# Output projection as seven block products in the MLP's pipeline, with sums and differences on GpSimd

## The chip, the cores and the metric

The kernel runs on one core of a Trainium2 chip. The metric is the device time of one execution in microseconds, as the median of several runs. The engines are TensorE (PE in the profile, PEld for its weight loads), VectorE (DVE), ScalarE (ACT), GpSimd (POOL) and SyncE (SP), which here only issues transfers. Each engine works through its own queue in order; semaphores tie the queues together.

## The reference, cut to what matters

Two decoder layers, model width D = 1024, T = 512 tokens, float32. In each layer:

```python
h = rmsnorm(x, norm_mix)
z = h @ w_in                       # attention, mLSTM and gate columns
mixed = sigmoid(g_a) * (att @ w_att_branch) + sigmoid(g_m) * (hm @ w_m_branch)
x = x + mixed @ w_out              # 1024 x 1024
u = relu(rmsnorm(x, norm_ffn) @ w_ff1)
x = x + (u * u) @ w_ff2            # 1024 -> 4096 -> 1024
```

The output projection is the line with `w_out`. It stands between the gated sum of the two branches, whose second product is the one with `w_m_branch`, and the norm ahead of the MLP.

## The kernel before, in words

**Precision.** Every float32 operand is split in two: a high part, the operand copied into the matmul type (on ScalarE), and a low part, operand minus high part (on VectorE). A product is three matmuls, high by high, high by low and low by high (`mm3`). In the names, `wh` and `wl` are the halves of a weight tile, `uh` and `ul` those of an activation tile of the MLP, `a` and `i` activation tiles.

**The mixer** (`mixer`, one call per layer) multiplies the normed input with pieces of `w_in`, does attention and the mLSTM beside that, and ends with the branch products. Weights come as 128x512 tiles of 256 KB through `chunk` (L164 to L192): a transfer into pool `wraw` (three buffers), the split on ScalarE (L190) and VectorE (L191) into pool `wsp` (four). `feat_steps` and `tok_steps` list the matmul groups of a product with the features or the tokens on the rows of its result; `weave` puts a list of side work between them at given places. For `w_m_branch` each result tile goes through `ev_m` (L786): VectorE multiplies it with the sigmoid (L788), adds the other branch (L789), and the sum is split. The output projection (L796 to L803) takes two column halves of eight weight tiles by four token blocks by three matmuls, 192 in a layer, and adds to the residual `xtok` (L799). The first half of the next norm's transposes is woven into its second column half.

**The MLP** (`mlp`) has four parts of 1024 hidden columns. FF1 of a part is four slots of 48 matmuls (`First`), each with two transfers of 512 KB (tile `f`). FF2 of a part is a 1024 x 1024 x 512 product done by 2 x 2 blocks with seven products in place of eight (`slots_of`): p1 to p7, each 24 matmuls in two halves of 12. It needs sums and differences of blocks. Of the weight blocks b11, b12, b21, b22 (512 KB tiles `raw`, two per block): d1 = b12 - b11, t2 = b22 - d1, b12 becomes b22 - b12, and b21 becomes b21 - t2. Of the activation blocks a11, a12, a21, a22 (tiles `u`, sums in `s`): s1 = a21 + a22, s2 = s1 - a11, s3 = a11 - a21, s4 = a12 - s2. All of these are VectorE operations on 128x1024 (`w_minus` L829, `u_op` L833). `w_split` (L820) and `u_split` (L837) make the halves, `gain` (L845) adds a product to the residual.

**The order.** The slots of all parts are one list. Ahead of half i of the list, the loads, splits and differences of the halves up to i + 5 are issued (`prepare`), so a weight half is prepared two and a half slots early. In parts 0 to 2 FF1 slots of the next part stand between FF2 products; in part 3 there are only the seven products. Memory comes from pools that are opened in turn at the start of `mixer` and of `mlp`, and are given back at its end; the pools of the next phase lie over those of the last, so that the first tile in such a place waits for the last use of what lay there.

Of the kernel before, what the change touches and what calls it, by code (L numbers as in the profile page):

```python
# [16 lines left out]
P = 128  # L17
# [11 lines left out]
NEG = -1.0e30  # L29
LN_EXP = "natural_log_exp_and_others"  # L30
# [3 lines left out]
def hybrid_kernel(ctx, tc, x, norm_mix, w_in, att_q_norm, att_k_norm, att_sinks, m_gate_bias,  # L34
# [87 lines left out]
    def g_ffn(l, k):  # L122
        return gcol[:, 16 + 8 * l + k:17 + 8 * l + k]
# [234 lines left out]

    def mixer(l, norm, late, order, phase):
# [4 lines left out]
        pool(phase, "act", 32)  # L364
        pool(phase, "tmp", 18)
        mid = pool(phase, "mid", 1)
# [132 lines left out]
        att_acts = [(slot(F32R), slot(F32R)) for _ in range(4)]  # L499
# [284 lines left out]
        mixed = [None] * KT  # L784
        for g in range(2):
            def ev_m(m, ps, g=g):  # L786
                i = 4 * g + m
                ve.tensor_tensor(sgm[g][m], sgm[g][m], ps, op=ALU.mult)  # L788
# [7 lines left out]
        for j in range(2):  # L796
            def ev_x(b, ps, j=j):
                xb = xtok[b // 2][j][:, b % 2, :]
                ve.tensor_tensor(xb, xb, ps, op=ALU.add)  # L799

            weave(tok_steps(mixed, lambda k, j=j: [w_out[l, k * P:(k + 1) * P, T * j:T * (j + 1)]], ev_x,
                            end_pair=j == 1),
                  norm.steps(0, 1.5, 0.5) if j else [])  # L803
        return norm

    def mlp(l, norm, late, phase):
# [22 lines left out]
        def w_minus(d, p, q):  # L829
            with tc.high_priority():  # L830
                ve.tensor_tensor(d, p, q, op=ALU.subtract)

        def u_op(d, p, q, op):  # L833
            with tc.high_priority():
                ve.tensor_tensor(d, p, q, op=op)
# [19 lines left out]
        class First:  # L855


            def __init__(self, part, q, which="f"):
                self.c0, self.q, self.which, self.w = 1024 * part + 256 * q, q, which, []

            def load(self, h):
                with tc.high_priority():
                    r = fr.tile([P, 4, 2 * P], F32, tag="f", name=nm("f"))
                    nc.sync.dma_start(r, w_ff1[l, 4 * h * P:4 * (h + 1) * P, self.c0:self.c0 + 2 * P]
                                      .rearrange("(k p) n -> p k n", p=P))
                self.w.append(w_split(r))

            def step(self, k):
                if k == 0:
                    self.ps = banks(self.which)  # L870
                hi, lo = self.w[k // 4]
                for m in range(2):
                    c = slice(m * P, (m + 1) * P)
                    mm3(self.ps[:, m, :], hi[:, k % 4, c], lo[:, k % 4, c], acts[k][0], acts[k][1], k == 0, k == KT - 1)
# [8 lines left out]
        def new_u():  # L883
            return [uraw.tile([P, 4, T], F32, tag=f"u{g}", name=nm("u")) for g in range(2)]
# [7 lines left out]
        def first_slot(part, q, u):  # L892
            f = First(part, q)
            return Slot(f.load, lambda h: [f.step(k) for k in range(4 * h, 4 * h + 4)], lambda: f.evac(u))
# [26 lines left out]
        def slots_of(part, u, nxt):  # L921
# [3 lines left out]
            end = part == 3  # L925
            b11, b12, b21, b22, t2 = ([None] * 2 for _ in range(5))

            def load(to, h, i, j):
                with tc.high_priority():
                    r0 = 1024 * part + (4 * i + 2 * h) * P  # L930
                    to[h] = raws.tile([P, 2, T], F32, tag="raw", name=nm("raw"))
                    nc.sync.dma_start(to[h], w_ff2[l, r0:r0 + 2 * P, j * T:(j + 1) * T]
                                      .rearrange("(k p) n -> p k n", p=P))
# [15 lines left out]
            def w6(h):  # L949
                return t2[h], lambda: w_minus(b12[h], b22[h], b12[h])  # L950
# [7 lines left out]
            def w2(h):  # L958
                load(b21, h, 1, 0)
                return b21[h], lambda: w_minus(b21[h], b21[h], t2[h])  # L960
# [19 lines left out]

            p1 = product("x", True, w1, lambda: a11, [(0, 0, False)])
            p5 = product("y", True, w5, s1, [(1, 1, False)])
            p6 = product("x", False, w6, s2, [(0, 1, False)])
            p3 = product("y", False, w3, s4, [(0, 1, end)])
            p7 = product("x", False, w7, s3, [(1, 1, end), (1, 0, False)])
            p2 = product("f" if end else "y", True, w2, lambda: a12, [(0, 0, end)])
            p4 = product("y", True, w4, lambda: a22, [(1, 0, end)])
# [4 lines left out]


        us = [new_u()]
        f01 = [First(0, 0, "f"), First(0, 1, "x")]
        for h in range(2):
            for f in f01:
                f.load(h)
        weave([(0.5, lambda k=k, f=f: f.step(k)) for k in range(KT) for f in f01], late + [(4.5, norm.columns), (6.5, lambda: rowf.append(norm.along()))])
        for f in f01:  # L1000
            f.evac(us[0])
        slots = [first_slot(0, 2, us[0]), first_slot(0, 3, us[0])]
        for part in range(4):
            if part < 3:
                us.append(new_u())
            slots += slots_of(part, us[part], us[part + 1] if part < 3 else None)
        halves = [(s, h) for s in slots for h in range(2)]
        preps = list(halves)
        side = nnorm.steps(1, 0.5, 0.5) if nnorm else []

        def prepare(n):
            while preps and len(halves) - len(preps) < n:
                s, h = preps.pop(0)
                s.prep(h)

        steps = []
        for i, (s, h) in enumerate(halves):
            def go(i=i, s=s, h=h):
# [7 lines left out]
            last = i >= len(halves) - 4  # L1026
            steps.append((1.0 if last else 0.0, go))
        weave(steps, side)
# [6 lines left out]
    for l in range(DEPTH):  # L1035
        with ExitStack() as phase:
            norm = mixer(l, norm, late, order, phase)
        late = norm.steps(1, 1.5, 0.5)
        with ExitStack() as phase:
            norm = mlp(l, norm, late, phase)  # L1040
        late = norm.steps(0, 1.5, 0.5) if norm else []
        order = [4, 5, 6, 7, 0, 1, 2, 3]
# [40 lines left out]
```

## Time and profile before

| | |
|---|---|
| Time, median of 3 runs | 1337.89 us (1336.92 to 1338.45) |
| Profiled execution, span from first to last instruction | 1335.6 us |
| TensorE busy | 1312.4 us (98%) |
| VectorE busy | 926.3 us (69%) |
| ScalarE busy | 666.4 us (50%) |
| GpSimd busy | 106.7 us (8%) |
| Mean granted TensorE clock | 0.999 |

The profiled execution's own time is its span; the median of the timed runs is 2.3 us above it. In a row of a group, the numbers behind the bar are the busy time of the group in us, the mean of one instruction in ns, and the idle time of the engine ahead of it with what ended it. In a row of a list in time order, the first number is the start and the second the duration, both in us. In a row of a window, the numbers are its length, then busy time and instructions of PE, PEld, DVE, ACT and POOL, the granted clock, the DMA engines' busy share and GB/s. In a wait row they are the total, the times and the longest. Matmuls overlap in the pipeline, so the time between two starts is what one costs. Line numbers of the first kernel are one to eight off those of the changed one: its L46 is L45 here, L191 and L192 are L190 and L191, L796 the add that was L789, L821 and L822 are L825 and L826, L827 is L831, L831 is L835, L837 and L838 are L841 and L842, L860 is L864.

### The profile page before, as it was taken

What the parts mean: (1) busy time and instruction counts of PE and PEld (TensorE: products, weight loads), DVE (VectorE), ACT (ScalarE), POOL (GpSimd) and SP (SyncE); (2) the same over time, 40 slices, a digit from 0 to 9 for tenths busy, and PEclk for the clock granted to TensorE, in tenths of its full rate; (3) what the DMA queues carried; (4) which work ended last, traced back from release to release, by engine and by line L of the source; (5) the groups of instructions that cost most, each with busy time, mean ns of one, the idle gap of its engine ahead of it and who ended that gap; (6) DMA issues with size and microseconds to landing.
All of it is one profiled execution on the core that took longest, in us unless ns stands there. A gap on an engine that the chain in (4) does not pass through costs nothing.

```text
span 1335.6 us, 16885 instructions
## 1 busy us (share of the span) xinstructions
PE 1312.4 (98%) x6106; PEld 1078.1 (81%) x6106; DVE 926.3 (69%) x1409; ACT 666.4 (50%) x1201; POOL 106.7 (8%) x215
## 2 busy tenths in 40 slices
PE   8999999999999999999999999999999999999998
PEld 6877788888788888888888777888887888888886
DVE  4688764474576876868947887554646778678687
ACT  5458765544334344343554687554434444344343
POOL 4512310000000000000015013000000000000000
PEclk9999999999999999999999999999999999999999
DMA  5322122421523133131024221243216242322211
GB/s 151 108 72 72 56 79 74 140 95 64 189 95 126 63 127 125 64 119 46 34 65 123 67 71 64 72 122 96 99 54 207 73 132 81 125 95 95 95 48 63
DMA packets 87282, 125.02 MB, mean 94 GB/s; under 512 B 8216, under 2 KB 45184, under 8 KB 87200
## 3 DMA queue, kind: packets, MB, share of 16 engines
q1 hardware_dynamic: 86240, 123.30, 29.3%
q8 instruction: 48, 0.79, 0.2%
q10 hardware_dynamic: 576, 0.53, 0.1%
q0 software_dynamic: 384, 0.13, 0.1%
q14 instruction: 34, 0.28, 0.1%
HBM read 121.84 MB, written 2.10 MB: 93 GB/s over the span
## 4 chain that ended last, share of the span: by engine, by line
PE 88%; DVE 6%; ACT 4%; issue 1%; DMA 1%; POOL 0%; ACTq 0%; SPq 0%; DVEq 0%; POOLq 0%
PE mm L45 82%; PE aux L45 4%; PE aux L49 2%; ACT t L574 1%; DVE wl L191 1%; ACT wh L190 1%; DVE t L561 1%; DVE t L611 0%; DMA w<-in_w_in_dram 0%; DVE t L201 0%; ACT wh L825 0%; DVE t L538 0%; ACT junk L287 0%; DVE t L579 0%; DMA grow<-in_norm_mix_dram 0%
## 5 line engine op out<-in xcount | busy, mean ns | idle before, releaser
L45 PE MATMUL mm<-i,wh 128*128 128x512 f32 x1664 | 522.6, 393 | 2.1 <-DVE a L661 1.2
L45 PEld LDWEIGHTS mm<-i,wh 128*128 128x128 f32 x1664 | 307.7, 188 | 65.8 <-DVE a L661 2.0
L45 PE MATMUL mm<-i,wl 128*128 128x512 f32 x832 | 324.8, 390 | 0.0
L191 DVE TENSOR_TENSOR wl<-w,wh 128x512 fp32r<-128x512 f32 (+1 forms) x208 | 140.4, 677 | 131.7 <-ACT wh L190 126.8
L190 ACT ACTIVATE wh<-w 128x512 fp32r<-128x512 f32 (+1 forms) x208 | 127.2, 612 | 146.9 <-PE mm L45 123.8
L825 ACT ACTIVATE wh<-raw 128x1024 fp32r<-128x1024 f32 x112 | 118.3, 1056 | 151.9 <-PE mm L45 116.4
L45 PEld LDWEIGHTS mm<-i,wl 128*128 128x128 f32 x832 | 156.2, 188 | 33.0 <-issue 0.5
L45 PE MATMUL mm<-wh,uh 128*128 128x512 f32 x448 | 174.5, 389 | 0.0
L45 PE MATMUL mm<-wh,ul 128*128 128x512 f32 x448 | 174.3, 389 | 0.0
L45 PE MATMUL mm<-wl,uh 128*128 128x512 f32 x448 | 174.3, 389 | 0.0
L826 DVE TENSOR_TENSOR wl<-raw,wh 128x1024 fp32r<-128x1024 f32 x112 | 135.9, 1219 | 37.8 <-ACT wh L825 37.4
L45 PE MATMUL mm<-wh,i 128*128 128x512 f32 (+1 forms) x512 | 149.8, 371 | 0.4 <-ACT wh L190 0.4
L825 ACT ACTIVATE wh<-f 128x1024 fp32r<-128x1024 f32 x64 | 67.2, 1056 | 118.8 <-PE mm L45 92.3
L45 PEld LDWEIGHTS mm<-wh,i 128*128 128x128 f32 x512 | 92.7, 189 | 15.9 <-ACT wh L190 0.8
L826 DVE TENSOR_TENSOR wl<-f,wh 128x1024 fp32r<-128x1024 f32 x64 | 77.7, 1221 | 30.3 <-ACT wh L825 30.1
L45 PEld LDWEIGHTS mm<-wh,ul 128*128 128x128 f32 x448 | 84.1, 188 | 17.5
L45 PEld LDWEIGHTS mm<-wh,uh 128*128 128x128 f32 x448 | 84.1, 188 | 17.4
L45 PEld LDWEIGHTS mm<-wl,uh 128*128 128x128 f32 x448 | 84.1, 188 | 17.3
L45 PE MATMUL mm<-wl,i 128*128 128x512 f32 (+1 forms) x256 | 94.7, 370 | 0.0
L879 DVE SCALAR_TENSOR_TENSOR u<-mm,t 128x1024 f32<-128x1024 f32 x32 | 39.1, 1222 | 69.2 <-PE mm L45 69.1
L849 DVE TENSOR_TENSOR x<-x,mm 128x1024 f32<-128x1024 f32 x64 | 77.2, 1217 | 13.6 <-PE mm L45 13.6
L45 PE MATMUL mm<-wh,a 128*128 128x512 f32 x256 | 81.4, 393 | 0.0
(214 smaller groups left out, 1619.0 us busy)
## 6 DMA issues: line engine op xcount, KB each, us to landing
w<-in_w_in_dram SPq DMA_DIRECT2D x128, 256.0 KB, 2.6
f<-in_w_ff_dram SPq DMA_DIRECT2D x64, 512.0 KB, 3.7
raw<-in_w_ff_dram SPq DMA_DIRECT2D x64, 512.0 KB, 3.5
w<-in_w_out_dram SPq DMA_DIRECT2D x32, 256.0 KB, 2.5
w<-in_w_att_branch_dram SPq DMA_DIRECT2D x16, 256.0 KB, 2.5
w<-in_w_m_branch_dram SPq DMA_DIRECT2D x16, 256.0 KB, 2.5
w<-in_w_in_dram SPq DMA_DIRECT2D x16, 128.0 KB, 2.1
out_dram<-x SPq DMA_DIRECT2D x8, 256.0 KB, 2.2
```

Source lines behind the costliest of these rows:

```text
L45: return nc.tensor.matmul(*args, **kw)
L49: return nc.tensor.transpose(*args)
L190: sc.activation(wh[:, :off], raw[:, :off], AF.Copy)
L191: ve.tensor_tensor(wl[:, :off], raw[:, :off], f32(wh[:, :off]), op=ALU.subtract)
L561: ve.copy_predicated(dst, tri_i.unsqueeze(1).to_broadcast([P, 2, P]), p4[:, :, 1, :])
L574: sc.activation(s3[:, i, :], s3[:, i, :], AF.Exp, bias=m[:, i:i + 1], accum_out=den[:, i:i + 1])
L825: sc.activation(hi, r, AF.Copy)
L826: ve.tensor_tensor(lo, r, f32(hi), op=ALU.subtract)
L849: ve.tensor_tensor(xh, xh, ps, op=ALU.add)
L879: ve.scalar_tensor_tensor(dst, self.ps, 0.0, rowf[0].unsqueeze(1).to_broadcast([P, 2, T]), op0=ALU.max, op1=ALU.mult)
```

## The change

The output projection is taken out of `mixer` and put at the start of `mlp`, as a list of seven products through the same `slots_of`, with `mixed` in the place of `u` and `w_out` in the place of `w_ff2`. Its order is p1, p2, p5, p6, p3, p7, p4. `mixed` is two tiles of 128x4x512 in a new pool `half`, which lives through the whole kernel, holds the attention's split result in the mixer, and also holds `u` of parts 1 and 3. The last add of `mixed`, all weight differences and all activation sums go to GpSimd. The last half of the norm's transposes is woven into the projection's last product and the first half into the first FF1 slots, which therefore take their rows in the order 4 to 7, 0 to 3. The pools of both phases are opened in another order.

```diff
+    half = ctx.enter_context(tc.tile_pool(name="half", bufs=1, reuse_waits="tile"))
...
-        pool(phase, "act", 32)
+        pool(phase, "act", 24)
+        mid = pool(phase, "mid", 1)
         pool(phase, "tmp", 18)
-        mid = pool(phase, "mid", 1)
...
-        mixed = [None] * KT
+        mixed = halves_of()
         for g in range(2):
             def ev_m(m, ps, g=g):
-                i = 4 * g + m
                 ve.tensor_tensor(sgm[g][m], sgm[g][m], ps, op=ALU.mult)
-                ve.tensor_tensor(prod[i], prod[i], sgm[g][m], op=ALU.add)
-                mixed[i] = split(prod[i])
+                gp.tensor_tensor(mixed[g][:, m, :], prod[4 * g + m], sgm[g][m], op=ALU.add)
...
-        uraw = pool(phase, "uraw", 2)
-        raws = pool(phase, "raws", 8)
-        uspl = pool(phase, "uspl", 2)
-        spl = pool(phase, "spl", 5)
-        pool(phase, "tmp", 2)
-        fr = pool(phase, "fr", 3)
+        uspl = pool(phase, "uspl", 2)
+        pool(phase, "tmp", 2)
+        uraw = pool(phase, "uraw", 1)
+        fr = pool(phase, "fr", 3)
+        raws = pool(phase, "raws", 8)
+        spl = pool(phase, "spl", 5)
...
         def w_minus(d, p, q):
             with tc.high_priority():
-                ve.tensor_tensor(d, p, q, op=ALU.subtract)
+                gp.tensor_tensor(d, p, q, op=ALU.subtract)
 
         def u_op(d, p, q, op):
             with tc.high_priority():
-                ve.tensor_tensor(d, p, q, op=op)
+                gp.tensor_tensor(d, p, q, op=op)
...
+            def w6(h):
+
+                def then():
+                    w_minus(b12[h], b22[h], b12[h])
+                    if part is None:
+                        w4_diff(h)
+
+                return t2[h], then
...
+            if part is None:
+                return [p1, p2, p5, p6, p3, p7, p4]
...
+        run(slots_of(None, mixed), norm.steps(1, 0.5, 0.5), 2)
+        us = [new_u(0)]
+        f01 = [First(0, 0, "f"), First(0, 1, "x")]
+        for h in (1, 0):
+            for f in f01:
+                f.load(h)
+        weave([(0.5, lambda i=i, k=k, f=f: f.step(i, k)) for i, k in enumerate(LATE_FIRST) for f in f01],
+              norm.steps(0, 1.5, 0.5)
+              + [(4.5, norm.columns), (6.5, lambda: rowf.append(norm.along()))])
...
-            norm = mixer(l, norm, late, order, phase)
-        late = norm.steps(1, 1.5, 0.5)
+            mixed = mixer(l, norm, late, order, phase)
         with ExitStack() as phase:
-            norm = mlp(l, norm, late, phase)
+            norm = mlp(l, mixed, phase)
```

How the queues stand now is shown at three places of layer 0; layer 1 reads alike. First SyncE's queue, where the transfers of the mixer's last weights end and those of the output projection begin, before:

```order
L180 DMA w_633_3082<-in_w_m_branch_dram 128x512 [waits DMAHW7_49,DVE_49]
L180 DMA w_636_3100<-in_w_m_branch_dram 128x512 [waits DMAHW0_49,DVE_49]
L180 DMA w_649_3144<-in_w_out_dram 128x512 [waits DMAHW1_49,DVE_49]
L180 DMA w_653_3163<-in_w_out_dram 128x512 [waits DMAHW2_49,DVE_49]
L180 DMA w_656_3181<-in_w_out_dram 128x512 [waits DMAHW3_49,DVE_49]
```

and after:

```order
L181 DMA w_624_3083<-in_w_m_branch_dram 128x512 [waits DMAHW5_49,DVE_49]
L860 DMA f_700_3471<-in_w_ff1_dram 128x4x256 [waits PE_49,Pool_49]
L932 DMA raw_632_3139<-in_w_out_dram 128x2x512 [waits Pool_49]
L860 DMA f_703_3477<-in_w_ff1_dram 128x4x256 [waits Pool_49]
L932 DMA raw_633_3141<-in_w_out_dram 128x2x512
L860 DMA f_706_3483<-in_w_ff1_dram 128x4x256
L932 DMA raw_636_3148<-in_w_out_dram 128x2x512 [waits DMAHW6_49]
L932 DMA raw_637_3150<-in_w_out_dram 128x2x512 [waits DMAHW7_49]
L932 DMA raw_640_3157<-in_w_out_dram 128x2x512 [waits DMAHW0_49,Pool_49]
L932 DMA raw_643_3163<-in_w_out_dram 128x2x512 [waits DMAHW1_49,Pool_49]
```

Before, a tile of w_out waited for a buffer that VectorE's split three tiles earlier had freed. Now an FF1 tile stands ahead of the first one, and its wait on PE is for the second-last matmul of w_m_branch, which read the memory that this tile takes. raw_632 and raw_636 are the two halves of b11, raw_633 and raw_637 of b12, raw_640 and raw_643 of b21.

Second, ScalarE's queue from the split of the last w_m_branch tile on, before:

```order
L190 ACTIVATE wh_637_3102<-w_636_3100 128x512
L200 ACTIVATE a_617_3022<-a_281_1392 128x512
L200 ACTIVATE a_619_3028<-a_282_1394 128x512
L190 ACTIVATE wh_650_3146<-w_649_3144 128x512
L200 ACTIVATE a_621_3034<-a_283_1396 128x512
```

and after:

```order
L191 ACTIVATE wh_625_3085<-w_624_3083 128x512 [waits DMAHW0_49,DVE_49,PE_49]
L837 ACTIVATE uh_630_3135<-u_597_2943 128x1024 [waits Pool_49]
L837 ACTIVATE uh_650_3177<-u_598_2944 128x1024 [waits PE_49,Pool_49]
L821 ACTIVATE wh_634_3143<-raw_632_3139 128x1024 [waits DMAHW2_49]
L821 ACTIVATE wh_638_3152<-raw_636_3148 128x1024 [waits DMAHW6_49]
L821 ACTIVATE wh_641_3159<-raw_640_3157 128x1024 [waits DMAHW0_49]
L837 ACTIVATE uh_659_3222<-s_629_3134 128x1024 [waits DVE_49,PE_49,Pool_49]
L821 ACTIVATE wh_644_3165<-raw_643_3163 128x1024 [waits DMAHW1_49]
```

u_597 and u_598 are the two tiles of `mixed`, wh_650 (before) and wh_634 (after) the first split of w_out. Before, tiles of `mixed` and of the weights were split in turn, eight by eight; now a copy of the second half of `mixed`, which product 2 uses, stands ahead of the first weight split. uh_659 is the split of s1.

Third, GpSimd's queue in the same place, after:

```order
L831 TENSOR_TENSOR s_629_3134<-u_597_2943,u_598_2944 128x1024 [waits PE_49,Activation_49,Pool_49]
L831 TENSOR_TENSOR u_597_2943<-u_597_2943 128x4x256 [waits Pool_49]
L827 TENSOR_TENSOR raw_632_3139<-raw_633_3141,raw_632_3139 128x1024 [waits DMAHW4_49,DMAHW2_49,DVE_49]
L827 TENSOR_TENSOR raw_636_3148<-raw_637_3150,raw_636_3148 128x1024 [waits DMAHW7_49,DMAHW6_49,DVE_49]
L827 TENSOR_TENSOR raw_649_3175<-raw_646_3169,raw_632_3139 128x1024 [waits DMAHW2_49,Pool_49]
L827 TENSOR_TENSOR raw_633_3141<-raw_646_3169,raw_633_3141 128x1024
L827 TENSOR_TENSOR raw_640_3157<-raw_640_3157,raw_649_3175 128x1024 [waits DMAHW0_49,DVE_49,Pool_49]
L831 TENSOR_TENSOR s_629_3134<-s_629_3134,u_597_2943 128x1024 [waits DVE_49]
L827 TENSOR_TENSOR raw_656_3200<-raw_653_3194,raw_636_3148 128x1024 [waits DMAHW3_49,DVE_49,Pool_49]
L827 TENSOR_TENSOR raw_637_3150<-raw_653_3194,raw_637_3150 128x1024
L827 TENSOR_TENSOR raw_643_3163<-raw_643_3163,raw_656_3200 128x1024 [waits DMAHW1_49,Pool_49]
L831 TENSOR_TENSOR s_629_3134<-u_598_2944,s_629_3134 128x1024 [waits DVE_49]
```

Before, GpSimd had nothing to do from the end of the mLSTM to the next layer. Its queue now holds, in this order and behind the eight adds of `mixed`, s1, s3, d1 of both halves, t2, b12 and b21 of the first half, s2, t2, b12 and b21 of the second half, then s4.

More of the change, by code (lines that the diff above doesn't have):

```diff
@@ L29 @@
 NEG = -1.0e30
+LATE_FIRST = [4, 5, 6, 7, 0, 1, 2, 3]
 LN_EXP = "natural_log_exp_and_others"
@@ L991, in slots_of, with run, prepare, go @@
             return [p1, f[0], p5, p6, f[1], p3, p7, f[2], p2, f[3], p4]
[L994 to L1018, printed above, removed]
+        def run(slots, side, last):
+            halves = [(s, h) for s in slots for h in range(2)]
+            preps = list(halves)
+            def prepare(n):
+                while preps and len(halves) - len(preps) < n:
+                    s, h = preps.pop(0)
+                    s.prep(h)
+            def go(i, s, h):
+                if i == 0 and s.acts_:
+                    s.acts_()
                 prepare(i + 5)
```

75 lines of the change are left out of this document (42 added, 33 removed).

## The prediction

> **What bounds the kernel now.** I read the busy totals and the chain of waits first, then TensorE's own waits, then the stages that the change touches as windows.
>
> ```profile
> PE 1312.4 (98%) x6106; PEld 1078.1 (81%) x6106; DVE 926.3 (69%) x1409; ACT 666.4 (50%) x1201; POOL 106.7 (8%) x215
> PE 88%; DVE 6%; ACT 4%; issue 1%; DMA 1%; POOL 0%; ACTq 0%; SPq 0%; DVEq 0%; POOLq 0%
> PE aux L49 <- DMA grow<-in_norm_mix_dram: 5.3, 1, 5.3
> PE aux L49 <- DVE t L561: 3.8, 6, 1.2
> PE mm L45 <- DVE a L661: 1.2, 2, 0.6
> ```
>
> TensorE works 98% of the span and 88% of the chain is its own. Its longest wait is the first load (5.3 us); after that no releaser costs it more than 3.8 us over the whole run. So a matmul removed is worth its full pitch, and equally a wait put ahead of TensorE is paid in full. The pitch, from two MLP matmuls and the window of layer 0's output projection:
>
> ```profile
> 655.03 0.39 PE L45 MATMUL mm<-wh,uh 128*128 128x512 f32 x1
> ...
> 661.38 0.39 PE L45 MATMUL mm<-wl,uh 128*128 128x512 f32 x1
> 278.80:322.40 43.60, 43.60 (x198) 36.10 (x198) 28.45 (x45) 16.00 (x26) 0.00 (x0) 1.00 0.31 98
> 333.50:691.00 357.50, 356.27 (x1587) 293.27 (x1587) 267.17 (x257) 156.02 (x180) 0.00 (x0) 1.00 0.30 98
> ```
>
> Between the first two rows lie 28 pitches, 6.35 / 28 = 0.227 us. The output projection's 192 matmuls take 43.6 us with TensorE never idle; the MLP (third row) idles 1.2 us in 357.5.
>
> Why is there no gap where `mixed` ends and the projection starts? Its weights come in pieces of 256 KB, asked for well ahead:
>
> ```profile
> L180 SPq DMA_DIRECT2D w<-in_w_out_dram x16: 327/328/328, 278.7 to 319.6; - x16
> DMA to landing us min/median/max: 2.4/2.5/2.8
> ```
>
> Sixteen issues from 278.7 to 319.6 are one per 2.72 us, 2.5 us each to land, three buffers deep: the supply keeps pace with use.
>
> **The change, part by part. Removed:** 24 matmuls per layer (seven products of 24 for 192), 48 in all: 48 x 0.227 = **-10.9 us**. Everything else on TensorE stays in number.
>
> **Added: a cold start of the projection, twice.** By the order of SyncE's queue nothing of w_out is asked for before the second-last w_m_branch matmul, as an FF1 load stands ahead of it that waits for that matmul. Call the end of w_m_branch T. What a burst of 512 KB tiles gives is seen at the start of the MLP before:
>
> ```profile
> 338.50 1.58 SPq L932 DMA_DIRECT2D raw<-in_w_ff_dram  x3
> L932 SPq DMA_DIRECT2D raw<-in_w_ff_dram x3: 378/379/469, 338.5 to 339.6; - x3
> DMA to landing us min/median/max: 3.9/4.5/6.2
> GB/s 0 0 0 0 0 0 0 119 279 348 168 377 406 369 344 324 360 301 285 317 385 410 389 391 377 360 369 379 373 356 336 295 354 365 254 70 119 150 330 346
> ```
>
> The first tile takes 3.9 us and the third lands at 339.6 + 6.2 = 345.8; the last row (0.5 us a slice from 336) settles near 350 GB/s, 1.5 us a tile. I take 3.9 us and 1.6 for each further tile, from T - 0.2. The first w_out block is the second transfer: T+5.3. Its other half is the sixth, T+11.7, since FF1 tiles and b12 are interleaved; the eighth (first block of product 2) lands at T+14.9, the ninth at T+16.5. Each then needs its two halves made:
>
> ```profile
> L825 ACT ACTIVATE wh<-raw 128x1024 fp32r<-128x1024 f32 x112 | 118.3, 1056 | 151.9 <-PE mm L45 116.4 <-issue 20.9 <-ACT wh L825 9.9
> L826 DVE TENSOR_TENSOR wl<-raw,wh 128x1024 fp32r<-128x1024 f32 x112 | 135.9, 1219 | 37.8 <-ACT wh L825 37.4
> L831 DVE TENSOR_TENSOR raw<-raw,raw 128x1024 f32<-128x1024 f32 x64 | 76.9, 1222 | 1.2
> L835 DVE TENSOR_TENSOR s<-u,u 128x1024 f32<-128x1024 f32 x8 | 9.8, 1225 | 0.0
> L788 DVE TENSOR_TENSOR a<-a,mm 128x512 f32<-128x512 f32 x16 | 10.6, 682 | 0.7 <-PE mm L45 0.4
> ```
>
> The last gating product needs 2 x 0.68 (L788) behind T; the last `mixed` add follows on GpSimd at T+3.6, and ScalarE's copy of the second half of `mixed` stands ahead of the first weight split, 1.06 more. The first split then ends T+6.4, so TensorE stands about **6.5 us** instead of none. The second half of product 1 can run at 11.7 + 1.06 + 1.22 = T+14.0 and ends T+16.5; product 2 starts when 14.9 + 2.3 = T+17.2 and, its second split being queued behind the copy of s1 which itself needs product 1's buffer, ends T+22.6. Gapless the two would end at T+10.9: 11.7 us lost by loads and splits alone.
>
> **Moved: sums and differences to GpSimd.** Per layer 8 adds of 128x512 and 60 operations of 128x1024. The nearest rows:
>
> ```profile
> L466 POOL TENSOR_TENSOR t<-a 128x512 f32<-128x512 f32 x8 | 8.4, 1086 | 504.0 <-ACT a L378 504.0
> L492 POOL TENSOR_TENSOR rp<-a,ct 128x128 f32<-128x128 f32 x8 | 4.3, 536 | 0.0
> L466 POOL TENSOR_TENSOR t<-a x8: 1037/1040/1230, 35.5 to 699.7; 128x512 f32<-128x512 f32 x8
> ```
>
> 1.04 us for 512 columns alone; 128 to 512 columns adds 0.50, so 1024 lie between 1.04 + 0.67 = 1.7 and 2 x 1.04 = 2.1. I take 2.0, nearest to doubling, against 1.22 on VectorE. In the projection GpSimd's chain (s1, s3, two d1, t2, b12, b21, s2, t2, b12, b21, s4: twelve times 2.0 = 24 us) runs beside 38.1 us of matmuls. Walked with the landings above, and with both engines free of each other, only s4 is late: product 3 starts about 1.8 to 2.4 us late, and product 4 ends at T+52.1. Less 168 x 0.227 = 38.1 that is **14.0 us of stall a layer**.
>
> **Costed at nothing.** The transposes and splits of the second norm move from FF1 and the old second column half into product 4 and FF1: the same number, and FF1 starts with the columns whose splits come from product 4. Their cover is product 4's 5.45 us (24 x 0.227); without it FF1's first matmul would wait for one ScalarE and one VectorE step, about 1.3 us by the L190 and L191 rows below. SyncE's fourth FF1 tile now queues behind five FF2 tiles which wait for buffers that the projection's splits free; those come free two products earlier, 10.9 us, against four landings of 1.6.
>
> **Do they run beside each other?** This is the largest unknown, and one place of the trace speaks on it:
>
> ```profile
> 711.35 0.18 DVE L405 TENSOR_TENSOR ig<-kvi,gbias 128x16 f32<-128x16 f32 x1
> 711.39 1.04 POOL L469 TENSOR_TENSOR t<-kvi 128x512 f32<-128x512 f32 x1 [10.49 <-ACT kvi L381]
> 711.44 1.02 DVE L407 TENSOR_TENSOR fg<-kvi,gbias 128x16 f32<-128x16 f32 x1
> L407 DVE TENSOR_TENSOR fg<-kvi,gbias x2: 1023/1024/1024, 50.6 to 711.4; 128x16 f32<-128x16 f32 x2
> ```
>
> Twin operations of 16 columns: the one begun before GpSimd's takes 0.18 us, the one begun just behind it 1.02, until GpSimd is done, and so in both layers. L466 in its turn reaches 1.23 us beside a VectorE split. I read that a VectorE operation with two inputs in SBUF and a GpSimd operation exclude each other. The Trainium skill says the same (SBUF — State Buffer, "Who interferes with whom": a VectorE instruction with two SBUF inputs contends with a GpSimd one that reads SBUF, and the second to issue is blocked until the first ends); by that rule, which these rows bear out, moving work to GpSimd frees nothing of VectorE's time. In the projection 21 splits of L826's and L842's kind (21 x 1.22 = 25.6) then share with 24 us of GpSimd: 49.6 us for 38.1 of matmuls. Walked in queue order, strictly alternating, `mixed` is done T+4.8, the first product still waits for the loads, product 2 ends T+26.9, product 5 33.2, product 6 (s2, t2) 40.9, product 3 (s4) 52.0, product 7 57.4, product 4 62.9: **24.8 us of stall a layer**. The bounds are 14.0 and 24.8; I take 24.8, the end that L407 is nearest to.
>
> In the MLP the same sharing is covered in parts 0 to 2: GpSimd 12 x 2.0 and VectorE 29 splits x 1.22 make 59 us under (168 + 4 x 48) x 0.227 = 81.7 of matmuls. Part 3 has no FF1 beside it: 49.6 under 38.1, with preparation running five halves ahead, about 10 us. I take 1 us a layer, **+2**, from 0 to 4 (gapless, or twice that).
>
> **The layer boundary.** The first w_in load of layer 1 now also waits for a matmul, the second-last of the MLP, where before it lay ready.
>
> ```profile
> L191 DVE TENSOR_TENSOR wl<-w,wh 128x512 fp32r<-128x512 f32 (+1 forms) x208 | 140.4, 677 | 131.7 <-ACT wh L190 126.8
> L190 ACT ACTIVATE wh<-w 128x512 fp32r<-128x512 f32 (+1 forms) x208 | 127.2, 612 | 146.9 <-PE mm L45 123.8
> w<-in_w_in_dram SPq DMA_DIRECT2D x128, 256.0 KB, 2.6
> ```
>
> 2.6 us to land, 0.61 and 0.68 for the split make 3.9; I set some 1.1 against it for the transposes that stand ahead of that matmul on TensorE, so **+2.8** (bounds 0 and 3.9).
>
> Sum against the profiled execution: 1335.6 - 10.9 + 49.6 + 2.0 + 2.8 = 1379.1. The median is 1337.9, 2.3 above that span: **1381 us**.
>
> **Rivals.** First, *the gain arrives*: loads start early enough, the new chain hides, and only -10.9 remains: **1327**. For it speaks the MLP's window, where the same seven products with 512 KB tiles idle TensorE hardly at all. Against it: there they are prepared five halves ahead, while here the load itself waits for T. It decides if w_out tiles land before T; price per layer 24 matmuls, and it breaks even when stalls stay under 5.4 us a layer, less than the 6.5 up to the first split.
>
> Second, *no exclusion*: GpSimd beside VectorE as if alone, stalls 2 x 14.0, boundary 2.8, part 3 free: 1335.6 - 10.9 + 28.0 + 2.8 + 2.3 = **1358**. For it: most splits of the before kernel have no GpSimd beside them, so L407 is thin evidence for large operations. It decides if L822's mean stays near 1.22.
>
> Third, *TensorE slows too*:
>
> ```profile
> 10.45 0.63 PE L45 MATMUL mm<-wl,i 128*128 128x512 f32 x1
> 10.88 0.63 PE L45 MATMUL mm<-wh,i 128*128 128x512 f32 x1
> ...
> 12.55 0.39 PE L45 MATMUL mm<-wl,i 128*128 128x512 f32 x1
> 12.78 0.40 PE L45 MATMUL mm<-wh,i 128*128 128x512 f32 x1
> ```
>
> At the start, behind its one long idle stretch, the pitch is 0.43, and from 12 us on 0.23. If the 6.5 us at T bring this back until TensorE is busy again for some 4 us, as there (7.9 to 12), each costs about 2 us; if every gap of the projection does, its 168 matmuls take up to twice 38.1 and, part of it lying in the gaps, at most some 10 us a layer are added: between 1385 and 1401, middle **1393**. Against it: the granted clock stands at 0.999 for the whole run, so the clock row didn't register the start either. The Trainium skill (TensorE: Matmul & The Clock Gate, the part on the clock states) puts the idle window at some 3.4 us and half speed until as much busy time has passed; the start agrees in size, and by it the sum would be near 1385 (two restarts).
>
> **How the numbers follow.** Exclusion with the alternation above 0.52; no exclusion, or little, 0.26; slower TensorE on top 0.13; gain arrives 0.06; stalls that just cancel it 0.03. Changes under 0.2% (2.7 us) can't be told from none. Faster 0.06, same 0.03, slower 0.91. The range has the second rival less its part of the loads that may land sooner (4 us a layer, so 8 below 1358) at its low end, and the third at its high end: **1350 to 1394**; the likeliest case alone is 1372 to 1386 (GpSimd at 1.7 takes up to 12 x 0.3 = 3.6 off a layer, at 2.1 adds 1.2; part 3 from 0 to 4).
>
> **What would show it.** (1) TensorE 48 matmuls fewer. (2) In each layer a wait of 6 to 8 us ahead of the first w_out matmul, released by ScalarE's split behind a DMA, and another of 3 to 6 us within products 1 and 2. (3) L827 and L831 on GpSimd at 1.7 to 2.1 us alone, up to 3.3 beside VectorE, and the splits L822 and L838 on VectorE with a mean well above 1.22; if they stay there, the second rival holds. (4) Matmuls of products 6 and 3 waiting for s2 and s4. (5) The projection 55 to 65 us long against 43.6. (6) A gap of 2 to 4 us at layer 1's first w_in matmul. I am wrong if the projection has no gap at T, or if parts 0 to 2 of the MLP stall by more than a few us.

## The result, and the profile after

The changed kernel takes 1406.81 us (median of 4 runs, 1404.91 to 1408.83), the kernel before 1337.41 beside it: the ratio is 1.052, with a 95% interval of 1.050 to 1.053. It is slower, as forecast, but by 69 us and not by the 43 of the forecast; the range ended at 1394.

The page of the changed kernel, its totals and its chain:

```profile
PE 1325.4 (94%) x6058; PEld 1080.5 (77%) x6058; DVE 976.8 (70%) x1291; ACT 675.3 (48%) x1195; POOL 473.2 (34%) x351
PE 42%; issue 26%; POOL 17%; DVE 11%; ACT 3%; POOLq 0%; DMA 0%; ACTq 0%; DVEq 0%
```

TensorE has 48 matmuls fewer (6106 to 6058) and is busy 94% instead of 98%. GpSimd went from nothing in the chain to 17% of it. VectorE lost 118 instructions and is busy *longer*, 976.8 us after 926.3, since an operation that another engine keeps out is recorded as busy (its rows follow below). TensorE's waits in the changed kernel, of which only the fifth and sixth were there before:

```profile
PE mm L46 <- DVE wl L822: 15.6, 6, 4.0
PE mm L46 <- ACT wh L821: 14.9, 2, 7.5
PE mm L46 <- ACT uh L837: 12.8, 4, 3.8
PE mm L46 <- DVE ul L838: 9.8, 7, 1.7
PE aux L50 <- DMA grow<-in_norm_mix_dram: 5.5, 1, 5.5
PE aux L50 <- DVE t L569: 4.3, 6, 1.5
```

To see where these lie, the span is cut at the starts of matmul groups: a stage "projection" from the end of w_m_branch to the first FF1 matmul, and a stage "part 3" from the first matmul behind the last FF1 slot (p4 of part 2, then part 3's seven products) to the next layer's first w_in matmul, or to the end. The windows of these stages in the kernel before, layer 0 and then layer 1:

```profile
293.60:340.60 47.00, 46.43 (x215) 38.12 (x214) 23.20 (x37) 18.69 (x32) 0.00 (x0) 1.00 0.20 66
626.50:671.80 45.30, 45.30 (x209) 37.68 (x208) 43.49 (x43) 26.62 (x34) 0.00 (x0) 1.00 0.16 54
953.70:1000.70 47.00, 46.45 (x215) 38.12 (x213) 23.21 (x37) 18.69 (x32) 0.00 (x0) 1.00 0.20 66
1286.60:1330.20 43.60, 43.60 (x193) 35.83 (x191) 38.83 (x35) 19.61 (x19) 0.00 (x0) 1.00 0.16 61
```

and in the changed kernel:

```profile
292.90:362.00 69.10, 47.78 (x185) 36.85 (x185) 59.96 (x38) 25.83 (x27) 41.38 (x16) 0.83 0.44 145
648.50:709.20 60.70, 52.23 (x220) 41.88 (x219) 48.99 (x34) 26.47 (x35) 28.02 (x10) 0.92 0.10 31
989.70:1058.60 68.90, 47.21 (x185) 36.29 (x185) 60.47 (x38) 25.82 (x27) 41.44 (x16) 0.85 0.43 145
1345.20:1398.10 52.90, 47.18 (x193) 37.54 (x191) 43.83 (x27) 19.25 (x19) 27.99 (x10) 0.94 0.14 50
```

The projection takes 22.1 and 21.9 us longer, part 3 15.4 and 9.3. That is 68.7 of the 67.9 us between the two spans (1335.6 and 1403.5); what lies between these stages moved by less than 1.5 us each. In the projection VectorE is busy 60 of 69 us, where it was 23 of 47.

One correction to the prediction's reading: its window 278.80:322.40 is where the w_out tiles were *asked for*. The matmuls run from 293.6 to 340.6 and take 47.0 us with the transposes among them. The sum did not rest on it, since the 10.9 us came from the pitch.

### The profile page after: what moved, and what is told of

It is laid out like the page before. It is cut to its first block, busy times and chain, and to the rows that moved or that the text cites. A ratio compares the mean times of both kernels' runs of the same rounds, so it can differ in the third digit from the quotient of the medians.

```text
span 1403.5 us, 16821 instructions
## 1 busy us (share of the span) xinstructions
PE 1325.4 (94%) x6058; PEld 1080.5 (77%) x6058; DVE 976.8 (70%) x1291; ACT 675.3 (48%) x1195; POOL 473.2 (34%) x351
## 4 chain that ended last, share of the span: by engine, by line
PE 42%; issue 26%; POOL 17%; DVE 11%; ACT 3%; POOLq 0%; DMA 0%; ACTq 0%; DVEq 0%
PE mm L46 36%; POOL raw L827 11%; POOL s L831 5%; PE aux L46 4%; DVE wl L822 3%; DVE ul L838 2%; PE aux L50 2%; DVE wl L192 1%; ACT t L582 1%; POOL u L796 1%; ACT uh L837 1%; DVE x L845 1%; DVE t L569 1%; DVE t L619 0%; ACT wh L821 0%
## 5 line engine op out<-in xcount | busy, mean ns | idle before, releaser
L827 POOL TENSOR_TENSOR raw<-raw,raw 128x1024 f32<-128x1024 f32 x80 | 226.4, 2848 | 393.7 <-DVE wl L822 392.5
L822 DVE TENSOR_TENSOR wl<-raw,wh 128x1024 fp32r<-128x1024 f32 x140 | 266.7, 1927 | 37.0 <-ACT wh L821 36.7
L46 PE MATMUL mm<-wh,uh 128*128 128x512 f32 x560 | 226.4, 404 | 27.7 <-ACT wh L821 14.9
L46 PE MATMUL mm<-wl,uh 128*128 128x512 f32 x560 | 225.6, 403 | 15.6 <-DVE wl L822 15.6
L46 PE MATMUL mm<-wh,ul 128*128 128x512 f32 x560 | 225.6, 403 | 9.8 <-DVE ul L838 9.8
L821 ACT ACTIVATE wh<-raw 128x1024 fp32r<-128x1024 f32 x140 | 144.3, 1051 | 138.7 <-PE mm L46 81.2
L191 ACT ACTIVATE wh<-w 128x512 fp32r<-128x512 f32 (+1 forms) x176 | 107.1, 609 | 117.2 <-PE mm L46 90.5
L46 PEld LDWEIGHTS mm<-wh,uh 128*128 128x128 f32 x560 | 109.7, 196 | 53.6 <-ACT wh L821 16.4
L46 PEld LDWEIGHTS mm<-wl,uh 128*128 128x128 f32 x560 | 109.4, 195 | 41.1 <-DVE wl L822 18.0
L46 PEld LDWEIGHTS mm<-wh,ul 128*128 128x128 f32 x560 | 109.4, 195 | 36.2 <-DVE ul L838 13.4
L822 DVE TENSOR_TENSOR wl<-f,wh 128x1024 fp32r<-128x1024 f32 x64 | 99.2, 1558 | 27.5 <-ACT wh L821 27.5
L837 ACT ACTIVATE uh<-s 128x1024 fp32r<-128x1024 f32 x30 | 31.8, 1059 | 130.8 <-POOL s L831 121.7
```

The lines of the kernel that those rows point to most:

```text
L46: return nc.tensor.matmul(*args, **kw)
L191: sc.activation(wh[:, :off], raw[:, :off], AF.Copy)
L821: sc.activation(hi, r, AF.Copy)
L822: ve.tensor_tensor(lo, r, f32(hi), op=ALU.subtract)
L827: gp.tensor_tensor(d, p, q, op=ALU.subtract)
L837: sc.activation(hi, t, AF.Copy)
```

## The experiments

All stage times below are cut as above; both layers are given where they differ.

**1. Everything back on VectorE.** Only the engine of the sums, the differences and the last add changes.

```diff
-                gp.tensor_tensor(mixed[g][:, m, :], prod[4 * g + m], sgm[g][m], op=ALU.add)
+                ve.tensor_tensor(mixed[g][:, m, :], prod[4 * g + m], sgm[g][m], op=ALU.add)
...
-                gp.tensor_tensor(d, p, q, op=ALU.subtract)
+                ve.tensor_tensor(d, p, q, op=ALU.subtract)
...
-                gp.tensor_tensor(d, p, q, op=op)
+                ve.tensor_tensor(d, p, q, op=op)
```

> The changed kernel with every sum and difference (and the last add of mixed) back on VectorE; nothing else differs, so the loads of w_out still start only at the end of w_m_branch. Theory (VectorE and GpSimd exclude each other, and a GpSimd operation is 2.4 us): splits return to 1.22 us, part 3 of the MLP is gapless again, the projection keeps the stalls of its late loads, some 10 to 14 us a layer, and the layer boundary keeps about 4: 1350 to 1362 us. Rival (late loads and the clock's restarts make the loss, the engine does not matter): 1390 us or more.

Measured: 1368.57 us, ratio to the kernel before 1.023 (1.021 to 1.024). So 38 of the 69 us were GpSimd's, and 31 are left, more than expected. Its windows, in the same order:

```profile
292.90:353.00 60.10, 45.64 (x177) 35.42 (x177) 55.21 (x53) 25.40 (x26) 0.00 (x0) 0.86 0.49 163
640.40:689.60 49.20, 46.98 (x222) 38.82 (x220) 43.96 (x42) 26.91 (x35) 0.00 (x0) 1.00 0.12 38
971.20:1030.20 59.00, 44.67 (x177) 34.60 (x177) 54.92 (x52) 25.39 (x26) 0.00 (x0) 0.88 0.49 164
1317.60:1361.30 43.70, 43.69 (x193) 35.86 (x191) 38.88 (x35) 19.64 (x19) 0.00 (x0) 1.00 0.17 61
```

Part 3 of the last layer is back at 43.7, and that of layer 0 is 3.9 us over the kernel before: the layer boundary, alone. The projection is still 12 to 13 us longer than 192 matmuls were, now with VectorE busy 55 of 60 us.

**2. GpSimd alone, in the kernel before.** The same two lines of differences and sums moved to GpSimd, the output projection left as it was.

> The kernel before, with only the differences of weight blocks and the sums of activation blocks of FF2 on GpSimd; the output projection stays 192 matmuls. Theory: parts 0 to 2 hide it, part 3 stalls some 8 to 12 us in each layer, so 1354 to 1362 us, and splits that meet GpSimd take up to 3.4 us. Rival (GpSimd hurts only where loads are late as well): within 3 us of the kernel before.

Measured: 1357.57 us, ratio 1.015 (1.013 to 1.016): 19.3 us. Both part 3 stages pay it:

```profile
626.40:681.70 55.30, 48.93 (x210) 39.08 (x210) 49.07 (x35) 26.19 (x34) 28.07 (x10) 0.94 0.15 48
1296.90:1349.90 53.00, 47.47 (x193) 37.66 (x191) 43.81 (x27) 19.28 (x19) 28.02 (x10) 0.94 0.14 50
```

10.0 and 9.4 us over the kernel before. Parts 0 to 2 hide it: from the first FF1 matmul to part 3 it is 286.1 and 285.8 us, before 285.8 twice.

**3. The gap at the start of the projection filled.** TensorE is given idle matmuls where it waits longest.

```diff
+        fill = aux()
+        for _ in range(54):
+            pe.matmul(fill, sel[:, 0, :], cm2, start=True, stop=True)
         run(slots_of(None, mixed), norm.steps(1, 0.5, 0.5), 2)
```

> The changed kernel with 54 idle matmuls per layer, whose result nobody reads, between w_m_branch and the first product, so that TensorE is not idle in the 12.5 us in which it waited there, and starts the product at full rate. Theory (the engines ahead of TensorE set the pace of the projection, so a restart at half rate is mostly swallowed by the next wait): within 3 us of the changed kernel, 1404 to 1408. Rival (the restarts add up): 2 to 4 us less in each layer, 1399 to 1403.

Measured: 1408.42 us (1405.15 to 1409.72), no change against the changed kernel. In the changed kernel the first product runs slowly, in this one at full rate; TensorE's list in time order, first of the changed kernel, then with the gap filled:

```profile
305.82 0.63 PE L46 MATMUL mm<-wh,ul 128*128 128x512 f32 x1
306.24 0.63 PE L46 MATMUL mm<-wh,uh 128*128 128x512 f32 x1
...
309.28 0.39 PE L46 MATMUL mm<-wh,ul 128*128 128x512 f32 x1
309.51 0.39 PE L46 MATMUL mm<-wh,uh 128*128 128x512 f32 x1
```

```profile
305.55 0.39 PE L46 MATMUL mm<-wh,uh 128*128 128x512 f32 x1
305.77 0.40 PE L46 MATMUL mm<-wl,uh 128*128 128x512 f32 x1
```

The time from one start to the next was 0.42 and is 0.22, and the projection is 70.0 and 70.3 us long after 69.1 and 68.9. The restart at half rate is real and cost nothing in this place: what TensorE loses in it, it would have spent waiting for the next split. Only the first gap of each projection was filled; the later ones still restart at half rate (the paragraph on the clock comes back to them).

**4. The loads of w_out early, GpSimd kept.** The pools of the MLP change places, so that the w_out and FF1 tiles lie over memory of the mixer that is free long before.

```diff
         uraw = pool(phase, "uraw", 1)
+        spl = pool(phase, "spl", 5)
         fr = pool(phase, "fr", 3)
         raws = pool(phase, "raws", 8)
-        spl = pool(phase, "spl", 5)
```

> The changed kernel with the MLP's pools in another order, so that the tiles of w_out and of FF1 lie over memory that is free long before the end of w_m_branch; GpSimd keeps all sums and differences. Theory (with loads in time the pair VectorE and GpSimd still needs some 3.35 us for each split and difference that meet): the projection falls by 4 to 8 us a layer only, 1390 to 1400 us. Rival (the late loads make the stall): the waits of products 1 and 2 vanish and the time falls by 12 us a layer or more, below 1385.

Measured: 1406.18 us (1404.72 to 1406.66): nothing, where I had expected at least 7. The loads of layer 0 did move, the first from 293.3 to 273.4, ahead of the projection, though the last, which waits for a buffer, only from 322.2 to 316.3:

```profile
L932 SPq DMA_DIRECT2D raw<-in_w_out_dram x8: 368/588/1757, 273.4 to 316.3; - x8
PE mm L46 <- ACT wh L821: 14.9, 2, 7.5
```

The first wait is as long as it was, and the projection takes 68.4 and 68.7 us after 69.1 and 68.9. ScalarE's queue still has the copy of the second half of `mixed` ahead of the first weight split, and that waits for GpSimd's last add. So the late loads, which the prediction priced at 11.7 us a layer, were not what decided.

**5. Both: VectorE and early loads.** Experiment 1, with the pools in the order uraw, tmp, uspl, spl, fr, raws; this also frees the memory of layer 1's first w_in tiles early.

> All sums and differences on VectorE as in the run before of that kind, and the MLP's pools in another order, so that the first tiles of w_out, and the first w_in tiles of layer 1, lie over memory that is free early. Theory (with GpSimd out of it, what is left of the projection's stall is VectorE's own queue: some 41 operations of 1.22 us and the last gating steps are 53 us behind the end of w_m_branch, for 41 us of matmuls and transposes): the projection goes from 60 to 54 to 57 us, the layer boundary loses its 4 us: 1350 to 1358 us. Rival (late loads are all that is left): the projection falls to 42 to 45 us, 1330 us or less, faster than the kernel before.

Measured: 1365.86 us (1360.85 to 1367.73), ratio 1.020 (1.018 to 1.022). The boundary is mended (45.3 in layer 0, as before). In layer 0 the first matmul of the projection now starts 1.1 us behind w_m_branch instead of 7.3, but the wait only moves. TensorE runs one matmul with the high half of the weight and then waits for the low half, which VectorE makes behind its last gating steps, s1, s3 and a split of `mixed`:

```profile
293.99 0.50 PE L46 MATMUL mm<-wh,uh 128*128 128x512 f32 x1 [0.92 <-ACT wh L821]
301.35 0.79 PE L46 MATMUL mm<-wl,uh 128*128 128x512 f32 x1 [6.86 <-DVE wl L822]
```

The projection as a whole does not get shorter:

```profile
292.90:354.40 61.50, 46.99 (x184) 36.93 (x184) 56.12 (x54) 25.99 (x27) 0.00 (x0) 0.86 0.24 78
641.00:686.30 45.30, 45.30 (x209) 37.66 (x208) 43.89 (x43) 26.00 (x32) 0.00 (x0) 1.00 0.20 65
968.70:1030.30 61.60, 47.04 (x186) 37.10 (x185) 56.16 (x54) 26.02 (x27) 0.00 (x0) 0.86 0.25 77
```

I had expected 54 to 57; it is 61.5, VectorE 91% busy. The last of the eight loads is still asked for late, at 318.0, as it needs a buffer, but VectorE waits only 0.3 us for it. The rival that only the loads were left falls.

**6. GpSimd where it is covered.** Experiment 5, with the differences and sums of parts 0 to 2 on GpSimd again.

> The kernel with VectorE and early loads, but with the differences and sums of the MLP's parts 0 to 2 on GpSimd; the projection and part 3 stay on VectorE. Theory (81.7 us of matmuls of a part cover the pair's work): within 3 us of the kernel with all on VectorE, though splits in these parts take up to 3.4 us. Rival (every exclusion is paid): 10 us or more slower than it.

Measured: 1363.80 us, beside 1365.86 with all of it on VectorE: no difference. Between FF1's first matmul and part 3 GpSimd is busy 100 us and TensorE loses nothing:

```profile
351.50:638.00 286.50, 286.27 (x1268) 236.00 (x1267) 205.06 (x154) 120.81 (x134) 99.96 (x36) 1.00 0.29 94
```

**7 and 8. The exclusion by itself.** The kernel before, with three GpSimd operations of 128x256 on a spare tile beside each difference and sum; nobody waits for them. In experiment 7 they are adds, in 8 memsets.

```diff
                 ve.tensor_tensor(d, p, q, op=ALU.subtract)
+                for _ in range(3):
+                    gp.tensor_tensor(spare, spare, spare, op=ALU.add)      # 8: gp.memset(spare, 0.0)
```

> The kernel before, with three added GpSimd adds of 128x256 on a tile of their own beside each difference and sum that VectorE does; nothing waits for them, so they run back to back at the start of the MLP. Theory (a VectorE operation with two SBUF inputs and a GpSimd operation that reads SBUF exclude each other): in that stretch splits take 1.9 to 2.0 us instead of 1.22, and the adds to the residual, which read one operand from PSUM, stay at 1.22. Rival (the longer durations of the changed kernel are the waiting for one another's results): all stay at 1.22.

> The same with three memsets of 128x256 in the place of the adds, which write SBUF and read nothing. Theory (the exclusion is one of reading): splits stay at 1.22 us. Rival (any GpSimd work excludes VectorE): 1.6 to 2.0 us.

The spare work ran earlier than I had placed it, from 209 us on in the mixer, so the splits it met are L191's, of 128x512. One run of each took 1346.59 and 1337.71 us (before: 1338.26). In the window from 210 to 250 us all three kernels have the same 13 splits. The groups of the kernel before:

```profile
L191 DVE TENSOR_TENSOR wl<-w,wh 128x512 fp32r<-128x512 f32 x13 | 9.0, 690 | 10.0 <-ACT wh L190 10.0
L661 DVE TENSOR_TENSOR a<-mm,t 128x512 f32<-128x512 f32 x4 | 2.6, 685 | 0.4 <-PE mm L45 0.3
```

with the adds:

```profile
L191 DVE TENSOR_TENSOR wl<-w,wh 128x512 fp32r<-128x512 f32 x13 | 11.6, 898 | 6.8 <-ACT wh L190 6.7
L661 DVE TENSOR_TENSOR a<-mm,t 128x512 f32<-128x512 f32 x4 | 2.6, 686 | 0.1
L835 POOL TENSOR_TENSOR spare<-spare 128x256 f32<-128x256 f32 x38 | 28.1, 739 | 3.0
```

and with the memsets:

```profile
L191 DVE TENSOR_TENSOR wl<-w,wh 128x512 fp32r<-128x512 f32 x13 | 9.0, 690 | 9.9 <-ACT wh L190 9.9
L835 POOL MEMSET spare<- 128x256 f32 x73 | 22.8, 313 | 4.2
L841 POOL MEMSET spare<- 128x256 f32 x36 | 11.3, 313 | 2.1
```

GpSimd is busy 36 and 34 of the 40 us. Beside its adds the splits take 898 ns, beside its memsets 690 as ever; L661, which reads one operand from PSUM, does not notice either. Nothing waits for a result of the spare tile, so the longer durations are the engines keeping each other out, here only where VectorE reads two operands from SBUF and GpSimd reads SBUF as well. The Trainium skill says so (SBUF — State Buffer, "Who interferes with whom": a VectorE operation with two SBUF inputs contends with a GpSimd one that reads SBUF, not with one that only writes); this trace agrees.

**9 and 10. Less work for VectorE in the projection.** Experiment 5, without the eight differences of weight blocks (9), and without these and the four activation sums (10).

```diff
+            def w_minus(d, p, q):
+                if part is not None:
+                    with tc.high_priority():
+                        ve.tensor_tensor(d, p, q, op=ALU.subtract)
...
-                    t2[h] = raws.tile([P, 2, T], F32, tag="raw", name=nm("raw"))
+                    t2[h] = b22[h] if part is None else raws.tile([P, 2, T], F32, tag="raw", name=nm("raw"))
```

> The kernel with all sums and differences on VectorE and early loads, and in the output projection the eight differences of weight blocks left out, so that its products take the plain blocks instead (the result of the projection is then another one). Theory (VectorE's queue sets the pace of the projection): 8 x 1.22 = 9.8 us less in each layer's projection, from 61.5 to 50 to 54 us. Rival (the pace is set by ScalarE's copies or by memory that comes free late): 57 us or more.

> The same, with three of the four activation sums left out as well as unneeded (s1, s2 and s4; each product takes a plain block), and s3 too, so 12 operations of 1.22 us fewer on VectorE than in the kernel with early loads. Theory: another 4 to 5 us less, 45 to 49 us, near the 41.6 us of matmuls and transposes. Rival (as above): no further change.

**11. More work for VectorE in the projection.** Experiment 5, with operations added that read each difference and write a spare tile.

```diff
                     ve.tensor_tensor(d, p, q, op=ALU.subtract)
+                    if part is None:
+                        for _ in range(3):
+                            ve.tensor_tensor(spare, d[:, 0, 0:2 * P], d[:, 0, 0:2 * P], op=ALU.add)
```

> The kernel with all sums and differences on VectorE and early loads, and behind each of the projection's eight differences three added VectorE operations of 128x256 on a tile that nobody reads, 24 x 0.41 = 9.9 us of VectorE per layer. Theory (VectorE sets the pace): the projection 6 to 10 us longer in each layer, 68 to 72 us. Rival (what waits are left are chains of single operations with VectorE idle between them): 3 us or less.

One run of each took 1344.93, 1339.44 and 1374.64 us (before: 1338.84). Layer 0's projection in experiments 9, 10 and 11:

```profile
293.30:343.10 49.80, 42.01 (x186) 34.45 (x185) 47.05 (x46) 26.28 (x27) 0.00 (x0) 0.93 0.26 87
```

```profile
293.30:340.40 47.10, 41.70 (x186) 34.26 (x185) 43.02 (x42) 26.20 (x27) 0.00 (x0) 0.96 0.29 91
```

```profile
292.70:357.30 64.60, 46.79 (x178) 36.38 (x178) 59.80 (x65) 25.30 (x26) 0.00 (x0) 0.82 0.18 56
```

Against experiment 5's 61.5 us with VectorE busy 56.1: 9.1 us less of VectorE made the stage 11.7 shorter, 13.1 less made it 14.4 shorter, and 3.7 more made it 3.1 longer. Experiment 11 missed its expected 6 to 10 us and lies at the edge of what its rival allowed, 3 us. Only 13 of the 24 added operations, 5.3 us of work, started within the stage, and the others behind it, where FF1 covers them. It is not a clean test either: the last load of w_out is asked for at 327.5 instead of 318.0, probably since the added operations read the differences and hold their buffers longer, and VectorE waits 0.8 us for it. So adding work shows the direction and not the size; that VectorE sets the pace rests on experiments 5, 9 and 10.

Removing a difference also removes a step between a load and its split, and t2 takes no buffer, so the last load is asked for at 284.5 instead of 318.0. Experiments 9 and 10 thus cut a chain as well as a queue, and part of their 1.1 to 1.3 us per microsecond of VectorE may be that.

A version that beats the kernel before was not found. The nearest ones with all sums and differences, experiments 5 and 6, are 2% slower, and experiment 10, without any in the projection, is only level with it: its first low half still keeps TensorE waiting 4.5 us. Preparing w_out's blocks ahead of the end of w_m_branch, when VectorE still has room, was not tried.

## Why the prediction was wrong in size

**Right: the 48 matmuls, the exclusion, the alternation.** TensorE has 48 fewer. The reading of L407 holds. VectorE and GpSimd in the changed kernel's projection, in time order:

```profile
308.78 12.29 POOL L827 TENSOR_TENSOR raw<-raw,raw 128x1024 f32<-128x1024 f32 x4 [1.16 <-DVE wl L822]
312.43 1.22 DVE L845 TENSOR_TENSOR x<-x,mm 128x1024 f32<-128x1024 f32 x1 [2.60 <-PE mm L46]
313.57 1.97 DVE L838 TENSOR_TENSOR ul<-s,uh 128x1024 fp32r<-128x1024 f32 x1
315.47 6.68 DVE L822 TENSOR_TENSOR wl<-raw,wh 128x1024 fp32r<-128x1024 f32 x2
```

GpSimd runs four differences in a row (12.29 us), and in that time the residual add with its PSUM operand takes its usual 1.22, while the two splits of L822 that follow take 3.34 each. Over the kernel:

```profile
L822 DVE TENSOR_TENSOR wl<-raw,wh 128x1024 fp32r<-128x1024 f32 x140 | 266.7, 1927 | 37.0 <-ACT wh L821 36.7
L827 POOL TENSOR_TENSOR raw<-raw,raw x80: 2367/2412/3392, 305.2 to 1383.7; 128x1024 f32<-128x1024 f32 x80
```

The rival "no exclusion" (1358) falls by this and by experiments 7 and 8. The rival "the gain arrives" (1327) falls by the first wait, 7.5 us in each layer where the prediction had 6.5.

**The step that failed: part 3.** The prediction set the exclusion's work of part 3, 49.6 us, against 38.1 of matmuls and let some 10 us of early preparation cover the difference: "I take 1 us a layer", from 0 to 4. It is 9.3 us in the last layer of the changed kernel, and 10.0 and 9.4 by experiment 2. The early preparation itself stood in the way, since GpSimd works in order. The last layer's part 3 begins at 1345.2:

```profile
1338.09 17.26 POOL L827 TENSOR_TENSOR raw<-raw,raw 128x1024 f32<-128x1024 f32 x6 [15.79 <-DVE wl L822]
1355.30 2.36 POOL L831 TENSOR_TENSOR s<-u,u 128x1024 f32<-128x1024 f32 x1
1358.80 0.50 PE L46 MATMUL mm<-wh,uh 128*128 128x512 f32 x1 [2.57 <-ACT uh L837]
1361.24 0.79 PE L46 MATMUL mm<-wh,ul 128*128 128x512 f32 x1 [1.70 <-DVE ul L838]
```

GpSimd does six weight differences before s1, which is done at 1357.7, and the product that uses s1 waits 2.6 us for its high half and 1.7 for its low half. From then on VectorE works without a pause until 1393.9, and TensorE waits 1.5 us more. These waits are 5.7 of the 9.3 us. For the other 3.6 TensorE is busy longer, 47.2 us where it was 43.6, with matmuls at half rate behind the second wait. VectorE had little room from the start: in the kernel before it is busy 38.8 of the 43.6 us of this stage, and the sum of 49.6 left out its eight adds to the residual.

Against the profiled execution's 1379.1 forecast and 1403.5 measured, 24.4 us apart, part 3 and the boundary hold 19.9: 15.4 + 9.3, less the 4.8 that the sum had for both. The boundary is 3.9 by experiment 1, for 2.8. The projection holds 5.3, and what lies between the stages gave 0.8 back.

**Mis-sized: GpSimd's operation.** "1024 lie between 1.7 and 2.1": it is 2.4 us alone, outside the bounds, and 3.3 beside a split, as the prediction had it. With 2.4 the pair's work in part 3 comes to 12 x 2.4 + 21 x 1.22 = 54.4 us, so the size explains part of that step too. The bounds were made from L466, which reads one tile twice (`t<-a`, 1.04 us). The add of `mixed`, which reads two, is the nearer kind, and the changed kernel has it:

```profile
L796 POOL TENSOR_TENSOR u<-a,a x16: 1255/1286/2248, 281.6 to 994.0; 128x512 f32<-128x512 f32 x16
```

1.26 us for the same 512 columns, and twice that is near the 2.4. The Trainium skill (GPSIMD Engine Reference, 3.1) has 4497 ns for an add of 2048 columns; half of it, 2.25 as an estimate, would have been nearer than my row.

**Near in size, wrong in cause: the projection.** The walk gave 24.8 us of stall a layer. With 3.4 us of transposes and the like (the kernel before's 47.0 over its 43.6 of matmuls), measured is 69.0 - 38.1 - 3.4 = 27.5, and the stage is 69 us long where the prediction named 55 to 65. But the walk let late loads make 11.7 of it in any case, and to come this near with a cause that is not there is luck in part. By experiments 4 and 5 mending the loads changes nothing, with GpSimd or without: with all of it on VectorE, that engine has 55 us of work behind the end of w_m_branch, whatever the loads do, for 41 us of TensorE. The figure was there to be added up before (21 splits, 12 sums and differences and 8 residual adds of 1.22 us, and the last gating steps), and the prediction added only the part that meets GpSimd.

**The clock.** The third rival's restart happened behind the long gaps (granted clock 0.83 in the projection) and the mean clock fell from 0.999 to 0.977. Behind the first gap it cost nothing, by experiment 3. The last slow stretch of the projection is another matter:

```profile
342.50:346.60 4.10, 4.08 (x10) 3.27 (x11) 4.10 (x4) 0.54 (x1) 0.00 (x0) 0.53 0.59 209
```

From here to the end of the stage TensorE waits for nothing, so what it loses here is probably paid: nine matmuls in 3.9 us where full rate needs 2.0, and likewise seven in 3.2 for 1.6 in layer 1. That is an estimate of up to 3.5 us in all. In part 3 TensorE's slow matmuls stand beside a VectorE that is full, so a faster TensorE would have had to wait for it; how much of the 3.6 us a layer was paid is not known. No run filled these gaps, so how much of the rival's 4 to 20 us came stays open. The Trainium skill (TensorE: Matmul & The Clock Gate, Part 1) has half rate for some 3.4 us of busy time behind an idle window; behind the first gap it lasted from 305.2 to 308.8 here, which agrees. By that rule the prediction had its sum near 1385 instead of 1381, for one restart a layer; the runs show that the first one is free.

## What to carry to other kernels

Before work moves from VectorE to GpSimd, count it on both together: where VectorE reads two operands from SBUF and GpSimd reads SBUF too, a split and a difference that take 2 x 1.22 us on VectorE take 3.34 us as a pair on the two engines. Saving matmuls by block products pays only if the engines that prepare operands have time in that very stage, so add up their work per stage and compare it with the matmuls left, after taking off what can be prepared ahead. Work that runs ahead in an in-order queue also stands ahead of what is needed first, as the six differences did before s1. A wait in front of the bounding engine is worth mending only if no other engine is full for the rest of the stage; otherwise it comes back one step later, as it did when the loads were brought forward.

## What the runs showed of the hardware that was not expected

- A GpSimd add of two tiles takes 1.26 us for 128x512 and 2.4 for 128x1024, against 1.04 for a product of one tile with itself at 128x512. The two kinds were not separated further.
- When splits and differences alternate, a pair takes 3.34 us and not 2.4 + 1.22 = 3.6.
- GpSimd's memsets, 34 of 40 us busy, leave VectorE's splits at 690 ns; its adds, 36 of 40 us busy, take them to 898.
- A restart of TensorE at half rate that lay ahead of another wait cost nothing: 1408.4 us with the first gap of each projection filled, 1406.8 without.
